# Token sums of a seven-product block FFN, formed before or after the transpose

## The chip, the cores and the metric

The kernel is one program on one core of a Trainium2 chip. The metric is the device time of one execution in microseconds (us). Engines are named as in the profile: PE (TensorE matmul) and PEld (its weight loads), DVE (VectorE), ACT (ScalarE), POOL (GpSimd), SP (SyncE, which issues most DMAs here).

## The reference, cut to what matters

One decoder layer for 1040 prompt rows (16 learned rows and 1024 tokens) and 64 sample rows, 1024 wide. It begins and ends with a SwiGLU half-step:

```python
def swiglu(x, w_gate, w_up, w_down):
    return (jax.nn.silu(x @ w_gate) * (x @ w_up)) @ w_down

def half_ffn(h, g_pre, g_post, w_gate, w_up, w_down):
    return h + 0.5 * rms_norm(swiglu(rms_norm(h, g_pre), w_gate, w_up, w_down), g_post)

h = half_ffn(h, ffn1...)                  # first half-step
...                                       # the token mixer: DeltaNet and attention
h = h + rms_norm(y @ w_out, g_mix_post)   # end of the mixer
h = half_ffn(h, ffn2...)                  # second half-step
```

Inner width is 2816. All is float32.

## The kernel before

**Seven products in place of eight.** Class `Ffn` does the products `x @ w_gate` and `x @ w_up` by a 2x2 block scheme. Tokens are cut into a left and a right half, the 1024 features into two halves of 512. Tile t = 0 to 3 (128 tokens each) is left and is paired with right tile t + 4; tile 8 is shorter, and its first half (40 tokens in the first half-step, 32 in the second) is left, its second half right. With x1, x2 the feature halves of a left tile and y1, y2 those of its right partner, the seven token operands are: 1 = x1, 2 = x2, 4 = y2, 5 = y1 + y2, 7 = x1 - y1, 6 = y1 + y2 - x1, 3 = x2 - 6. Each is kept feature-major (128 features x 4 x tokens) as a pair of fp32r tiles, high part and rest; a name such as `x60l` is operand 6, token part 0, the low tile. A product is three matmuls: high by high, rest by high, high by rest.

**A place.** `place` (L203 to L211) makes one operand of one tile: four PE transposes of 128 x 128 into a PSUM tile `tr` (L208; pool of four), an ACT copy that makes the high part (L210) and a DVE subtract that makes the rest (L211). `left` (L217) does two places for a left tile. `right` (L224) first forms the sums token-major (128 tokens x 512), two on DVE and two on POOL (L230), in place in the two token tiles and a tile `sum`, and then does five places. That is 2 x 5 + 5 x 5 = 35 places in each half-step.

**First half-step.** `tiles_in` (L1902) loads the token tiles, normalizes them (ACT square L81, POOL L82 and L83, DVE L90) and runs `left` and `right`. Left tiles have buffers of their own; right tiles 4, 5, 6, 7, 8 share two buffers, so tile 6 goes into that of tile 4. The PE work is `first`, the first products with operands 1 and 2, in two token parts, and then `start(1)`; `weave` puts the steps of `tiles_in` between its matmuls at given shares of the way (L1947 to L1951).

**End of the mixer and second half-step.** Class `Merge` walks the tiles in the order 0, 4, 1, 5, 2, 8, 6, 3, 7. For each it does the output projection (`tile_`, two PSUM tiles `dn` of 512 columns, 24 matmuls each, copied out by ACT at L1830 or L1827), adds the residual and normalizes (`finish`), and weaves into the projection of tile i the places of tile i - 2 (`feed`, L1781). The output tile is one of three:

```python
o = c.t(*((self.first, [P, H, P], F32R, "yh") if i % 3 == 0 else (self.pool, [P, H, P], F32R, "o")))
```

`self.first` has one buffer of that name and `o` two, so tile 5's output goes into the buffer of tile 0, and tile 8's into that of tile 1: the left partners of tiles 4 and 5, whose places were woven in just before. `h_d` in the profile is the store of a tile ahead of its last normalization, which is done in place. Tiles 2 and 8 are stored to DRAM (`kept`) and loaded again by `rest` (L1787), which does the places of 6, 3, 8 and 7 between the first matmuls of the second half-step (L2030 to L2034).

**Order.** PE follows the order in which the code emits, weaves included. The other engines' instructions are put in order by a scheduler; each engine then runs its own queue strictly in order. A token tile's buffer is free for its next user when the last reader or writer of the old one is done.

Of the kernel before, what the change touches and what calls it, by code (L numbers as in the profile page):

```python
# [18 lines left out]
P = 128  # L19
D = 1024  # L20
# [150 lines left out]
class Ffn:  # L171
# [31 lines left out]
    def place(self, psum, p, i, o, src, n):  # L203

        c, nc = self.c, self.nc
        ps = c.t(psum, [P, 4, P], tag="tr")
        for k in range(4):
            nc.tensor.transpose(ps[:, k, :n], src[:n, k * P:(k + 1) * P], c.ident[:n, :n])  # L208
        hi, lo = (x[:, :, o:o + n] for x in self.X[p][i])
        nc.scalar.copy(hi, ps[:, :, :n])  # L210
        nc.vector.tensor_tensor(out=lo, in0=ps[:, :, :n], in1=f32(hi), op=ALU.subtract)  # L211
# [4 lines left out]

    def left(self, psum, x, t):  # L217

        i, o, n = self.where(t)
        for p, h in ((1, 0), (2, 512)):  # L220
            self.place(psum, p, i, o, x[:, h:h + 512], n)
            yield

    def right(self, pool, psum, x, y, t):  # L224

        nc = self.nc
        i, o, n = self.where(t)
        x1, x2, y1, y2 = x[:n, 0:512], x[:n, 512:], y[:n, 0:512], y[:n, 512:]
        s = self.c.t(pool, [P, 512], tag="sum", bufs=2)[:n]
        op = lambda e, out, a, b, o: e.tensor_tensor(out=out, in0=a, in1=b, op=o)  # L230
        op(nc.vector, s, y1, y2, ALU.add)
        op(nc.vector, y1, x1, y1, ALU.subtract)
        op(nc.gpsimd, x1, s, x1, ALU.subtract)
        op(nc.gpsimd, x2, x2, x1, ALU.subtract)
        for p, src in ((4, y2), (5, s), (7, y1), (6, x1), (3, x2)):
            self.place(psum, p, i, o, src, n)
            yield
# [1453 lines left out]
class Merge:  # L1691
# [76 lines left out]
    def finish(self, t, n, o, dump):  # L1768
# [8 lines left out]
        if t in (2, 8):  # L1777
            self.kept[t] = c.t(self.f2_d, [P, D], tag="kept", bufs=2)
            nc.sync.dma_start(self.kept[t][:n], o[:n])

    def feed(self, t):  # L1781

        if t in (4, 5):
            return self.f2.right(self.pool, self.f2.ptr, self.o[t - 4], self.o[t], t), 5
        return self.f2.left(self.f2.ptr, self.o[t], t), 2

    def rest(self):  # L1787
# [5 lines left out]
        for x, src in ((x2, self.kept[2]), (x8[:n], self.kept[8][:n]), (y8[:n], self.kept[8][n:2 * n])):  # L1793
            self.nc.sync.dma_start(x, src)
        yield from right(pool, self.f2.ptr, x2, self.o[6], 6)
        yield from self.feed(3)[0]
# [371 lines left out]
```

## Time and profile before

| | us |
|---|---|
| median of 3 runs | 2686.57 (2686.21 to 2691.09) |
| profiled execution | 2687.11 |
| its span | 2685.2 |
| mean granted TensorE clock | 0.991 |
| PE busy in the span | 2604.9 (97%) |
| DVE, ACT, POOL busy | 1556.6 (58%), 1127.4 (42%), 1290.1 (48%) |

The span is the time from the first to the last instruction that the profiler sees; the 1.9 us between it and the execution's time lie outside. Rows of the timeline give the start, the duration, the engine, the line of the code, output<-inputs and the size; in brackets stands how long the engine was idle before and what released it.

### The profile page before, as it was taken

The numbers are of one execution on the slowest core, as the hardware profiler recorded it, in microseconds if no ns is written. First come the engines' busy times: TensorE is split into PE (matmuls) and PEld (weight loads), VectorE is DVE, ScalarE is ACT, GpSimd is POOL, SyncE is SP. The second block draws the span as 40 slices with busy tenths as digits, with TensorE's granted clock in tenths as the row PEclk, the third lists the DMA queues.
The fourth block names the chain that finished last, engine by engine and source line by source line (L and its number), as shares of the span: only waits on it lengthen the run. The fifth ranks groups of instructions, "written<-read, shape, count | busy, mean of one in ns | idle before, by whom it ended". The sixth has DMA issues, their size and how long they took to land. (4 is left out here: it accounts for less than half of the span.)

```text
span 2685.2 us, 49482 instructions
## 1 busy us (share of the span) xinstructions
PE 2604.9 (97%) x19053; PEld 2483.4 (92%) x19053; DVE 1556.6 (58%) x2295; ACT 1127.4 (42%) x2720; POOL 1290.1 (48%) x1223
## 2 busy tenths in 40 slices
PE   7999999999989998999999999998999999999998
PEld 7999999999988997888889999997789999999998
DVE  7656565545676669945454444443556656554566
ACT  6333343422145633566444444454443334334221
POOL 6656555445535733433343333344556555554471
PEclk9999999999999999999999999999999999999999
DMA  4343343667544753454333333334433434338764
GB/s 162 115 156 144 133 166 116 242 227 253 189 141 140 221 164 111 124 176 118 98 100 90 91 97 95 99 107 142 141 125 138 154 128 160 123 137 318 242 224 143
DMA packets 229568, 406.46 MB, mean 151 GB/s; under 512 B 59750, under 2 KB 121350, under 8 KB 229046
## 3 DMA queue, kind: packets, MB, share of 16 engines
q1 hardware_dynamic: 209030, 324.75, 37.2%
q10 hardware_dynamic: 20304, 78.56, 7.4%
q8 instruction: 150, 2.46, 0.4%
q14 instruction: 84, 0.69, 0.1%
HBM read 264.36 MB, written 140.53 MB: 151 GB/s over the span
## 5 line engine op out<-in xcount | busy, mean ns | idle before, releaser
L132 PE MATMUL gu<-xh,wl 128*128 128x512 f32 (+3 forms) x1456 | 495.4, 340 | 0.0
L128 PE MATMUL gu<-xh,wh 128*128 128x512 f32 (+3 forms) x1456 | 492.9, 339 | 0.0
L130 PE MATMUL gu<-xl,wh 128*128 128x512 f32 (+3 forms) x1456 | 492.2, 338 | 0.0
L282 POOL TENSOR_TENSOR wl<-T,wh 128x512 fp32r<-128x512 f32 x246 | 330.5, 1349 | 321.6 <-ACT wh L281 247.5
L492 PE MATMUL y<-hb,wh 128*128 128x256 f32 (+2 forms) x2528 | 430.5, 290 | 2.9 <-DVE acc L503 1.3
L282 POOL TENSOR_TENSOR wl<-raw,wh 128x512 fp32r<-128x512 f32 x200 | 282.8, 1422 | 254.3 <-ACT wh L281 193.3
L492 PEld LDWEIGHTS y<-hb,wh 128*128 128x128 f32 x2528 | 365.8, 188 | 4.3 <-DVE acc L503 1.8
L281 ACT CAST wh<-T 128x512 fp32r<-128x512 f32 x246 | 152.5, 620 | 368.7 <-PE B L316 115.5
L128 PEld LDWEIGHTS gu<-xh,wh 128*128 128x128 f32 x1456 | 278.0, 191 | 16.6 <-issue 0.9
L130 PEld LDWEIGHTS gu<-xl,wh 128*128 128x128 f32 x1456 | 278.0, 191 | 16.5 <-issue 0.4
L132 PEld LDWEIGHTS gu<-xh,wl 128*128 128x128 f32 x1456 | 278.0, 191 | 16.4 <-issue 0.4
L492 PE MATMUL y<-hb,wl 128*128 128x256 f32 (+2 forms) x1264 | 271.7, 288 | 0.2 <-POOL wl L282 0.2
L281 ACT CAST wh<-raw 128x512 fp32r<-128x512 f32 x200 | 122.3, 620 | 280.7 <-PE C L316 84.0
L503 DVE TENSOR_TENSOR acc<-acc,y 128x552 f32<-128x552 f32 (+4 forms) x216 | 144.9, 679 | 138.8 <-PE y L492 138.3
L765 POOL TENSOR_TENSOR wl<-raw,wh 128x1024 fp32r<-128x1024 f32 x60 | 145.5, 2425 | 159.9 <-ACT wh L764 130.4
L492 PEld LDWEIGHTS y<-hb,wl 128*128 128x128 f32 x1264 | 207.0, 188 | 0.5 <-POOL wl L282 0.5
L256 DVE TENSOR_TENSOR T<-raw,raw 128x512 f32<-128x512 f32 x124 | 119.9, 972 | 113.3 <-POOL wl L282 113.3
L1548 POOL TENSOR_TENSOR f<-f,mhalf 128x1 f32<-128x1 f32 (+1 forms) x72 | 54.5, 757 | 128.0 <-DVE f L1546 126.5
L267 DVE TENSOR_TENSOR T<-raw,T 128x512 f32<-128x512 f32 x62 | 64.5, 1042 | 65.1 <-POOL wl L282 64.7
L923 DVE SCALAR_TENSOR_TENSOR cv<-pc,cw,cv 128x1131 f32<-128x1131 f32 x48 | 66.8, 1393 | 31.0 <-POOL cv L920 30.7
L256 DVE TENSOR_TENSOR T<-raw,T 128x512 f32<-128x512 f32 x62 | 63.2, 1028 | 33.2 <-POOL wl L282 33.1
L1064 DVE TENSOR_TENSOR la<-la,ltmp 72x14 f32<-72x14 f32 (+37 forms) x76 | 75.3, 991 | 1.4
(592 smaller groups left out, 7304.8 us busy)
## 6 DMA issues: line engine op xcount, KB each, us to landing
hb<-hid SPq DMA_DIRECT2D x71, 552.0 KB
hb<-hid SPq DMA_DIRECT2D x71, 544.0 KB
hid<-hs ACTq DMA_DIRECT2D x69, 552.0 KB
hid<-hs ACTq DMA_DIRECT2D x69, 544.0 KB
raw<-in_w_in_dram SPq DMA_DIRECT2D x58, 512.0 KB
raw<-in_ffn_w_gate_dram SPq DMA_DIRECT2D x100, 256.0 KB
raw<-in_ffn_w_up_dram SPq DMA_DIRECT2D x94, 256.0 KB
raw<-in_ffn_w_down_dram SPq DMA_DIRECT2D x88, 256.0 KB
```

Source lines behind the costliest of these rows:

```text
L128: nc.tensor.matmul(ps, wh, xh, start=first and i == 0, stop=False)
L130: nc.tensor.matmul(ps, wh, xl, start=False, stop=False)
L132: nc.tensor.matmul(ps, wl, xh, start=False, stop=last and i == n - 1)
L256: pin(self.nc.vector.tensor_tensor(out=b[name], in0=b[x], in1=b[y], op=ALU.subtract))
L267: nc.vector.tensor_tensor(out=s, in0=b["21"], in1=s, op=ALU.subtract)
L281: self.nc.scalar.copy(hi, s)
L282: self.nc.gpsimd.tensor_tensor(out=lo, in0=s, in1=f32(hi), op=ALU.subtract)
L492: self.nc.tensor.matmul(self.view(ps[d], (i,)), w[x][:, d * P:(d + 1) * P], hb[:, y, lo:hi], start=j + x + y == 0, stop=j == len(items) - ...
L503: dve = lambda out, x, y: nc.vector.tensor_tensor(out=out, in0=x, in1=y, op=ALU.add)
L765: nc.gpsimd.tensor_tensor(out=lo, in0=raw, in1=f32(hi), op=ALU.subtract)
L923: nc.vector.scalar_tensor_tensor(out=cv, in0=pc[:, w:w + PADW], scalar=self.cw[:, j, w:w + 1], in1=cv, op0=ALU.mult, op1=ALU.add)
L1064: nc.vector.tensor_tensor(out=a[:n, 0:j, j + 1:size], in0=a[:n, 0:j, j + 1:size], in1=t, op=ALU.add)
```

## The change

Both half-steps get it at once. `left` copies each transposed half back on chip with one more ACT copy (L230 of the changed kernel), over the half of the token tile that it came from, so that the buffer of a left tile then holds it feature-major. `right` transposes y2 and y1 alone. It forms 7 = x1 - y1 and 6 = y2 - 7 on DVE, over the buffer of the right tile, and 5 = x1 + 6 and 3 = x2 - 6 on POOL, over the buffer of the left tile (all L239), all feature-major; their high and low parts are made from these SBUF tiles by the same ACT copy (L213) and DVE subtract (L214) as before. A right tile has 2 places with transposes in place of 5, and 2 steps to be woven in. The weaves are spread anew, and `kept` holds tiles 2 and 8 feature-major, stored from `left` and not from `finish`; the right half of tile 8 is stored by itself (`kept_y`).

```diff
     def left(self, psum, x, t):
         i, o, n = self.where(t)
-        for p, h in ((1, 0), (2, 512)):
-            self.place(psum, p, i, o, x[:, h:h + 512], n)
+        for p, h, own in zip((1, 2), (0, 512), self.halves(x, n)):
+            ps = self.turned(psum, x[:, h:h + 512], n)
+            self.place(p, i, o, ps)
+            self.nc.scalar.copy(own, ps)
             yield
...
-        s = self.c.t(pool, [P, 512], tag="sum", bufs=2)[:n]
...
-        op(nc.vector, s, y1, y2, ALU.add)
-        op(nc.vector, y1, x1, y1, ALU.subtract)
-        op(nc.gpsimd, x1, s, x1, ALU.subtract)
-        op(nc.gpsimd, x2, x2, x1, ALU.subtract)
-        for p, src in ((4, y2), (5, s), (7, y1), (6, x1), (3, x2)):
-            self.place(psum, p, i, o, src, n)
-            yield
+        y2 = self.turned(psum, y[:, 512:], n)
+        self.place(4, i, o, y2)
+        yield
+        y1 = self.turned(psum, y[:, 0:512], n)
+        op(nc.vector, s3, x1, y1, ALU.subtract)
+        op(nc.vector, s2, y2, s3, ALU.subtract)
+        op(nc.gpsimd, x1, x1, s2, ALU.add)
+        op(nc.gpsimd, x2, x2, s2, ALU.subtract)
+        self.place(7, i, o, s3)
+        self.place(6, i, o, s2)
+        self.place(5, i, o, x1)
+        self.place(3, i, o, x2)
+        yield
...
-        weave((first, 0, 1, 49), (steps_of(tr, 10), 0.1, 0.9, 10))
-        weave((f1.start(1, False), 0, 1, 49), (steps_of(tr, 10), 0.1, 0.9, 10))
+        weave((first, 0, 1, 49), (steps_of(tr, 4), 0.1, 0.9, 4))
+        weave((f1.start(1, False), 0, 1, 49), (steps_of(tr, 4), 0.05, 0.85, 4))
...
-        weave((steps_of(first, 48), 0, 1, 48), (steps_of(rest, 7), 0.25, 0.95, 7))
-        weave((first, 0, 1, 49), (steps_of(rest, 5), 0.1, 0.8, 5))
-        weave((f2.start(1, False), 0, 1, 49), (steps_of(rest, 5), 0.1, 0.8, 5))
+        weave((steps_of(first, 48), 0, 1, 48), (steps_of(rest, 4), 0.25, 0.9, 4))
+        weave((first, 0, 1, 49), (steps_of(rest, 2), 0.2, 0.7, 2))
+        weave((f2.start(1, False), 0, 1, 49), (steps_of(rest, 2), 0.1, 0.6, 2))
```

**First place: the loads of tiles 6, 7 and 8 in the first half-step.** SP's queue before, from the last early weight tile on; the brackets name whom a load waits for. `x_416`, `x_515` and `x_614` are tiles 6, 7 and 8.

```order
L249 DMA raw_492<-in_ffn_w_up_dram 128x512 [waits DMAHW7_49,Pool_49]
L249 DMA raw_494<-in_ffn_w_up_dram 128x512 [waits DMAHW0_49,Pool_49]
L1911 DMA x_416<-in_x_prompt_dram 128x1024 [waits DMAHW1_49,DVE_49,PE_49]
L1911 DMA x_515<-in_x_prompt_dram 128x1024 [waits DMAHW2_49,DVE_49,PE_49]
L1915 DMA x_614<-in_x_sample_dram 24x1024 [waits DMAHW3_49,DVE_49,PE_49]
L1916 DMA x_614<-in_meta_tokens_dram 16x1024 [waits DMAHW4_49]
```

The same rows of the changed kernel (tiles 6, 7 and 8 are `x_413`, `x_493` and `x_578`):

```order
L264 DMA raw_470<-in_ffn_w_up_dram 128x512 [waits DMAHW7_49,Pool_49]
L264 DMA raw_472<-in_ffn_w_up_dram 128x512 [waits DMAHW0_49,Pool_49]
L1933 DMA x_413<-in_x_prompt_dram 128x1024 [waits DVE_49,DMAHW1_49,PE_49,Pool_49]
L1933 DMA x_493<-in_x_prompt_dram 128x1024 [waits DVE_49,DMAHW2_49,PE_49,Pool_49]
L1937 DMA x_578<-in_x_sample_dram 24x1024 [waits DVE_49,DMAHW3_49,PE_49,Pool_49]
L1938 DMA x_578<-in_meta_tokens_dram 16x1024 [waits DMAHW4_49]
```

Each load now waits for POOL too: the buffer of tile 4 is read by POOL's sums, where before PE's transposes and a DVE sum were its last readers. POOL's queue at this place before, where `x_36` and `x_37` are tiles 0 and 1, `x_159` is tile 4 and `x_161` tile 5:

```order
L230 TENSOR_TENSOR x_36_139<-sum_355,x_36_139 128x512
L230 TENSOR_TENSOR x_36_139<-x_36_139 128x512
L230 TENSOR_TENSOR x_37_141<-sum_424,x_37_141 128x512
L282 TENSOR_TENSOR wl_555<-raw_492,wh_554 128x512
L230 TENSOR_TENSOR x_37_141<-x_37_141 128x512
L282 TENSOR_TENSOR wl_607<-raw_490,wh_606 128x512
```

And in the changed kernel:

```order
L297 TENSOR_TENSOR wl_521<-raw_470,wh_520 128x512
L297 TENSOR_TENSOR wl_569<-raw_468,wh_568 128x512
L239 TENSOR_TENSOR x_36_139<-x_36_139,x_159 128x512 x2
L297 TENSOR_TENSOR wl_615<-raw_472,wh_614 128x512
L239 TENSOR_TENSOR x_37_141<-x_37_141,x_161 128x512 x2
```

The sums of tile 4 (x2: two in a row) moved behind two weight splits `wl` (of the third and second weight tile) that stood behind both of them before, and they now read what PE has transposed and DVE has subtracted.

**Second place: the end of tile 4's places in Merge.** ACT's queue before. `o_21931` is tile 1's output, `yh_22017` tile 5's, in the buffer that was tile 0's; `tr` are the transposed halves.

```order
L210 CAST x40h_21779<-tr_22057 128x4x128
L210 CAST x50h_21794<-tr_22068 128x4x128
L81 ACTIVATE res_21998,rn_22007<-o_21931 128x1024
L210 CAST x70h_21804<-tr_22078 128x4x128
L210 CAST x60h_21789<-tr_22088 128x4x128
L1830 COPY yh_22017<-dn_22018 128x512
L210 CAST x30h_21774<-tr_22099 128x4x128
L1830 COPY yh_22017<-dn_22044 128x512
```

ACT's queue in the changed kernel, where `yh_21687` is tile 0's buffer, `o_21789` tile 4's, `yh_21949` tile 5's output in the buffer of `yh_21687`:

```order
L213 CAST x40h_21709<-tr_21987 128x4x128
L213 CAST x70h_21734<-o_21789 128x4x128
L213 CAST x60h_21719<-o_21789 128x4x128
L213 CAST x50h_21724<-yh_21687 128x4x128
L213 CAST x30h_21704<-yh_21687 128x4x128
L1853 COPY yh_21949<-dn_21950 128x512
L1853 COPY yh_21949<-dn_21976 128x512
```

The first copy of tile 5's output out of `dn` stood ahead of the copy for operand 3; it now stands behind it, and takes the buffer from which operands 5 and 3 are made. DVE's queue at the same place before:

```order
L619 SCALAR_TENSOR_TENSOR o_21931<-o_21931,rp_22000,g_mix_norm_post_21838 128x1024
L211 TENSOR_TENSOR x40l_21780<-tr_22057,x40h_21779 128x4x128
L211 TENSOR_TENSOR x50l_21795<-tr_22068,x50h_21794 128x4x128
L211 TENSOR_TENSOR x70l_21805<-tr_22078,x70h_21804 128x4x128
L90 SCALAR_TENSOR_TENSOR o_21931<-o_21931,rn_22007,g_ffn_norm_pre_21847 128x1024
L211 TENSOR_TENSOR x60l_21790<-tr_22088,x60h_21789 128x4x128
L211 TENSOR_TENSOR x30l_21775<-tr_22099,x30h_21774 128x4x128
```

And in the changed kernel:

```order
L214 TENSOR_TENSOR x40l_21710<-tr_21987,x40h_21709 128x4x128
L90 SCALAR_TENSOR_TENSOR o_21861<-o_21861,rn_21939,g_ffn_norm_pre_21777 128x1024
L239 TENSOR_TENSOR o_21789<-yh_21687,tr_22002 128x512
L239 TENSOR_TENSOR o_21789<-tr_21987,o_21789 128x512
L214 TENSOR_TENSOR x70l_21735<-o_21789,x70h_21734 128x4x128
L214 TENSOR_TENSOR x60l_21720<-o_21789,x60h_21719 128x4x128
L214 TENSOR_TENSOR x50l_21725<-yh_21687,x50h_21724 128x4x128
L214 TENSOR_TENSOR x30l_21705<-yh_21687,x30h_21704 128x4x128
```

The two sums (L239) stand behind the normalization L90 of tile 1 (`o_21861`), which waits for that tile's store, and ahead of all that is made from them. Before, tile 4's sums were ahead of all its places. PE meets the copy at its tile 2 (`dn_22046`), six matmuls behind the transposes of y1 (`tr_22002`):

```order
L132 MATMUL dn_21976<-xh_3933_21415,yl_21856 128x512
L207 MATMUL tr_22002<-ident_62,o_21789 128x128 x4
L128 MATMUL dn_21976<-xh_3981_21582,yh_21857 128x512
L130 MATMUL dn_21976<-xl_3982_21583,yh_21857 128x512
L132 MATMUL dn_21976<-xh_3981_21582,yl_21856 128x512
L128 MATMUL dn_21976<-xh_3981_21582,yh_21857 128x512
L130 MATMUL dn_21976<-xl_3982_21583,yh_21857 128x512
L132 MATMUL dn_21976<-xh_3981_21582,yl_21856 128x512
L128 MATMUL dn_22046<-xh_3892_21263,yh_21945 128x512
```

Before, one more place of tile 4 stood in these matmuls. The same pattern holds for tile 5's places and the output of tile 8, which goes into tile 1's buffer.

56 lines of the change are left out of this document (33 added, 23 removed).

## The prediction

> **What bounds the kernel now.** I read the page's engine rows first, then PE's waits, then the timeline at the stages in which the places lie (13 to 70 us, and 1870 to 1985 us).
>
> ```profile
> span 2685.2 us, 49482 instructions
> PE 2604.9 (97%) x19053; PEld 2483.4 (92%) x19053; DVE 1556.6 (58%) x2295; ACT 1127.4 (42%) x2720; POOL 1290.1 (48%) x1223
> PE tr L208 <- DVE x L90: 10.9, 2, 9.5
> PE tr L208 <- DVE x41l L211: 2.2, 1, 2.2
> PE tr L208 <- POOL x-8_45_157 L230: 1.8, 2, 0.9
> ```
>
> PE is the bound: it is busy for 97% of the span, and its waits on the places are few (total, count, longest): the first normalization, 2.2 us on `x41l`, 1.8 us on POOL's sums of tile 8. So what comes off PE's queue comes off the time, one for one, as long as no new wait takes its place; the other engines count only where PE waits for them.
>
> **What goes: thirty places.** Three places of each right tile, five right tiles, two half-steps. The price of one, from the timeline of tile 4 in Merge:
>
> ```profile
> 1883.64 0.40 PE L132 MATMUL dn<-xh,yl 128*128 128x512 f32 x1
> 1883.87 0.39 PE L128 MATMUL dn<-xh,yh 128*128 128x512 f32 x1
> 1884.10 0.60 PE L208 MATMUL tr<-ident,o 128*128 128x128 f32 x4
> 1884.46 0.48 PE L130 MATMUL dn<-xl,yh 128*128 128x512 f32 x1
> 1884.77 0.39 PE L132 MATMUL dn<-xh,yl 128*128 128x512 f32 x1
> ```
>
> Matmuls follow one another by 0.23 us. Four transposes hold the queue for 0.36 (1884.10 to 1884.46), and the matmul behind them takes 0.31 to the next, 0.08 more than usual: 0.44 us a place. Thirty are 13.2 us: 6.6 in the first half-step, 2.6 in Merge (tiles 4 and 5), 4.0 in the start of the second half-step. POOL's and DVE's work stays about what it was, and ACT gains 20 copies of about 0.6 (below), 12 us on an engine that is busy for 42%; I cost them at nothing, except where a chain runs through ACT.
>
> **What comes in: a longer chain behind the second transpose.** Before, the sums were made before the places, and a place was over when PE, ACT and DVE had read `tr`. Now, behind the transposes of y1, stand DVE twice, POOL twice, then ACT and DVE for operands 5 and 3; and the buffers of both token tiles are busy until that is done. The rows of the old sums (min/median/max in ns):
>
> ```profile
> L230 DVE TENSOR_TENSOR x<-x,x x4: 685/934/1668, 28.4 to 48.4; 128x512 f32<-128x512 f32 x4
> L230 POOL TENSOR_TENSOR x<-sum,x x4: 1292/1454/2278, 29.3 to 49.7; 128x512 f32<-128x512 f32 x4
> L230 POOL TENSOR_TENSOR o<-o x2: 1282/1284/1287, 1908.8 to 1971.4; 128x512 f32<-128x512 f32 x2
> ```
>
> So I take 0.68 for a DVE sum (0.60 for one right behind another), 1.25 to 1.28 for a POOL sum; the bounds above are 1.67 and 2.28, where the two engines ran beside each other. Who waits for the end of that chain? Two kinds of buffer.
>
> **Merge, tile 5's output.** It goes into tile 0's buffer, from which operands 5 and 3 of tile 4 are now made.
>
> ```profile
> 1889.12 0.60 PE L208 MATMUL tr<-ident,yh 128*128 128x128 f32 x4
> 1889.42 1.28 DVE L90 SCALAR_TENSOR_TENSOR o<-o,rn,g_ffn_norm_pre 128x1024 f32<-128x1024 f32 x1 [0.48 <-DMA h_d<-o]
> 1889.75 0.59 ACT L1830 COPY yh<-dn 128x512 f32<-128x512 f32 x1 [0.78 <-PE tr L208]
> 1890.23 0.59 ACT L210 CAST x30h<-tr 128x512 fp32r<-128x512 f32 x1
> 1890.39 0.19 PEld L128 LDWEIGHTS dn<-xh,yh 128*128 128x128 f32 x1 [0.41 <-ACT yh L1830]
> 1890.62 0.68 DVE L211 TENSOR_TENSOR x60l<-tr,x60h 128x512 fp32r<-128x512 f32 x1
> 1891.22 0.68 DVE L211 TENSOR_TENSOR x30l<-tr,x30h 128x512 fp32r<-128x512 f32 x1
> ```
>
> Now: PE's last transposes end, the copy out of `dn` follows, and PE goes on with tile 2 at 1890.39, after 0.41 us of waiting. With the change, PE has six matmuls (1.4 us) between the transposes of y1 and tile 2's first. The copy stands behind: two DVE sums (1.28), two POOL sums (2.5), `x30h` (0.59), `x30l` (0.68), the copy itself, and handovers: 6.5 us from the end of the transposes, so PE waits for at least 4.7 us with nothing else in the way. DVE has L90 of tile 1 ahead of the sums, and that waits for a store that lands at about 1889.4; it ends at 1890.7 at the earliest. From there 1.3 + 2.5 + 0.6 + 0.7 + 0.6 and handovers end at about 1896.7, where PE without the wait would be at about 1889.0 (three places earlier than now). I take 7.7 us, 0.4 of which is there already: +7.3; bounds 4.3 and 9 (slower sums).
>
> **Merge, tile 8's output.** The same with tile 1's buffer and operands 5 and 3 of tile 5.
>
> ```profile
> 1912.60 0.59 ACT L1827 COPY o<-dn 128x512 f32<-128x512 f32 x1 [0.98 <-PE tr L208]
> 1913.24 0.50 PE L128 MATMUL dn<-xh,yh 128*128 128x512 f32 x1 [0.25 <-ACT o L1827]
> ```
>
> Here four matmuls (0.9 us) stand between the transposes of y1 and tile 6's first, and no store: 5.1 by the chain, less about 0.7 of waits that go (0.25 here, 0.44 at this tile's first place): +4.4, bounds 3.5 and 7 (normalization of tile 2 stands in POOL's queue ahead of the sums).
>
> **First half-step, tile 6.** Its load goes into tile 4's buffer.
>
> ```profile
> 33.90 5.10 SPq L1911 DMA_DIRECT2D x<-in_x_prompt_dram  x2
> 37.38 1.06 ACT L81 ACTIVATE dump<-x 128x1024 bf16<-128x1024 f32 x1 [0.54 <-DMA x<-in_x_prompt_dram]
> 38.89 0.55 POOL L83 TENSOR_TENSOR rn<-rn,mhalf 128x1 f32<-128x1 f32 x1
> 39.65 1.28 DVE L90 SCALAR_TENSOR_TENSOR x<-x,rn,g_ffn_norm_pre 128x1024 f32<-128x1024 f32 x1
> 41.24 0.28 PE L316 MATMUL A<-x10h,wh 128*128 128x256 f32 x1
> 42.89 0.30 PE L316 MATMUL A<-x11h,wh 128*128 128x296 f32 x1
> 43.03 0.60 PE L208 MATMUL tr<-ident,x 128*128 128x128 f32 x4
> 59.27 0.41 PE L208 MATMUL tr<-ident,x 40*128 40x40 f32 x4 [0.33 <-DVE x L230]
> 60.53 0.44 PE L208 MATMUL tr<-ident,x-8_45_157 40*128 40x40 f32 x4 [0.86 <-POOL x-8_45_157 L230]
> 61.88 0.44 PE L208 MATMUL tr<-ident,x-8_45_157 40*128 40x40 f32 x4 [0.90 <-POOL x-8_45_157 L230]
> ```
>
> Now the load is issued at 33.90, lands after 3.5, and square, POOL and L90 end at 40.9, 2 us before PE wants the tile. With the change the load waits for POOL's second sum: y1 of tile 4 transposed, 1.3 + 2.5 + 3.5 (load) + 1.2 (square) + 0.8 (POOL) + 1.3 (L90) and handovers are 11 us. PE has only 39 matmuls and two places from there to tile 6's transposes. At 0.13 a matmul (41.24 to 42.89 is 13 of them) and 0.44 a place, with the hold of y1's own transposes, that is 6.3 us. The wait is 4.7 at the least and 6 as I take it, with a weight split (1.28) ahead on POOL. Tile 7 has the time; tile 8 is one load later still, and POOL's queue has tile 7's sums ahead of its normalization. Now PE waits 2.1 us in all at tile 8 (0.33, 0.86 and 0.90); I expect 2 to 4 more, less what its three places give, and take +2. The own copies of tiles 2 and 3 delay the start by about 0.4. Sum: -6.6 + 6 + 2 + 0.4 = +1.8 before the clock.
>
> **Start of the second half-step.** A gap that PE has now should go:
>
> ```profile
> 1955.18 0.68 DVE L230 TENSOR_TENSOR yh<-yl,yh 32x512 f32<-32x512 f32 x1 [3.00 <-DMA yl<-kept]
> 1957.80 1.01 PE L208 MATMUL tr<-ident,yl 128*128 128x128 f32 x4 [2.23 <-DVE x41l L211]
> 1955.00:1958.00 3.00, 0.77 (x7) 0.60 (x7) 2.82 (x4) 0.59 (x1) 2.01 (x1) 0.98 0.00 0
> 1958.00:1961.00 3.00, 3.00 (x16) 3.00 (x15) 2.13 (x4) 2.13 (x3) 2.92 (x3) 0.50 0.02 5
> ```
>
> DVE's sum of tile 8 waits for the load of `kept` at the head of its queue, and `x41l` of tile 6, and PE with it, behind that. In the changed order that sum stands behind tile 8's transposes, after all of tile 6 and 3. So about 2.4 us of gap go. The last two rows are windows (length, busy of PE, PEld, DVE, ACT and POOL, granted clock, DMA): after the gap PE is busy at a clock of 0.50 for some 3.3 us, which costs 1.65. That goes too: -4.1. New waits are possible, the store and load of tile 8 in pieces of 128 bytes among them, for which no row exists; I bound them by 0 and by today's gap (2.4) and take 1.0, the nearer row for a load that is wanted later.
>
> **The clock.** By the same two rows each new wait of over 2.4 us costs 1.65 us behind it: three such waits, +5. The Trainium skill (TensorE: Matmul & The Clock Gate, part 1 on what is actually happening) says that the clock halves after an idle window of about 3.4 us and comes back after as long a busy one. The 0.50 rows agree with the way back, but not with the way down: 2.4 us without work were enough here, so the row decides.
>
> **The sum.** First half-step +1.8 + 1.65; Merge -2.6 + 7.3 + 4.4 + 3.3; start of the second -4.0 - 4.1 + 1.0. That is +3.5 + 12.4 - 7.1 = +8.8. The profiled execution took 2687.1, which is 0.5 above the median of 2686.6; against the median this gives 2695.4, and I say 2695. Waits at their upper bounds (+1.7, +2.6, +2 at tile 8, +1.4) give about 2703; at their lower bounds (-3, -0.9, -1.3, -1) about 2689.
>
> A rule of the Trainium skill speaks against the change: SBUF — State Buffer, who interferes with whom, has DVE with two SBUF inputs and POOL lock each other out for a whole instruction. The subtracts that make operands 7, 6, 5 and 3 now read SBUF twice; before, one input was `tr`. The DVE row above (685 to 1668 for two SBUF inputs, beside POOL) bears it out; by the rule a POOL sum on each of the three chains would wait for one subtract, some 0.7 each, an estimate, and the sum would be 2 us higher. It stays within the range.
>
> **Rivals.**
> - *Only the places count.* The copies and loads turn out early enough, because something ahead of the chain (tile 1's store, the splits on POOL) is done sooner, and PE has no new wait over a microsecond. Then -13.2 - 4.1 and up to 3 of small waits: about 2672. For it: ACT and DVE are busy for half of the span at most. Against it: the three floors (4.3, 3.5, 4.7) come from durations alone, with no queue in them. It decides for faster from the point at which the three waits, clock included, come to under 8 us in sum; I expect 22.7 (7.3 + 4.4 + 6 + 5).
> - *The floors alone.* Each wait at its floor, and the clock not halved, or once: -13.2 - 4.1 + 4.3 + 3.5 + 4.7 + 3 + 1.65 = 0: about 2686, no change that can be told.
> - *The chain is worse.* POOL's sums at 2.28 and behind normalizations, tile 8's load late in both half-steps: 2704 to 2710.
>
> **How the numbers follow.** A measurement of this kernel can tell about 0.2%, 5.4 us: faster is below 2681.2, slower above 2692.0. My forecast (2689 to 2703) has a chance of 0.50, of which 0.06 lies under 2692; the floors 0.20, of which 0.03 are under 2681; only the places 0.20; the worse chain 0.10. So slower 0.54, same 0.23, faster 0.23. The range takes in about half of the case of the places alone and leaves out most of the last: 2673 to 2704; the likeliest case's own range is 2689 to 2703.
>
> **What would show it.** In the changed profile: the PE row of transposes at 160 instead of 280 instructions; a wait of PE on the copy of L1853 of 5 to 9 us at about 1889, one on L1850 of 4 to 7 some 20 us later, one on L90 of 5 to 7 at about 40 us, each with some 3 us at a clock of 0.50 behind it; no wait on `x41l`. If these waits are absent or under 2 us, the forecast is wrong by the sum of the floors, and the time is at 2672 to 2676.

## The result and the profile after

The changed kernel takes 2718.47 us (2716.25 to 2721.21, 4 runs), the kernel before 2688.66 (2686.21 to 2691.09, 4 runs) beside it: a ratio of 1.0111, with a 95% interval of 1.0094 to 1.0129. It is 30 us slower. The forecast was 2695 and slower; the direction holds, the size does not, and the time lies above the range. In all that follows, the ratios leave out one execution of 6510 us, in the experiment with everything together, which no trace here explains.

From the page of the changed kernel come the first two rows; the other four are PE's waits (line waited at, whose work is waited for, total us, times, longest).

```profile
span 2717.2 us, 49246 instructions
PE 2603.2 (96%) x18933; PEld 2481.7 (91%) x18933; DVE 1565.2 (58%) x2295; ACT 1137.0 (42%) x2740; POOL 1289.2 (47%) x1223
...
PE tr L207 <- DVE x L90: 20.4, 3, 9.7
PE dn L128 <- ACT o L1850: 8.7, 1, 8.7
PE tr L207 <- issue: 7.7, 1, 7.7
...
PE dn L128 <- ACT yh L1853: 5.8, 1, 5.8
```

PE has 120 instructions less, 19053 to 18933, as the thirty places of four transposes give. Yet its busy time is only 1.7 us shorter. Four waits are new: 7.6 of the 20.4 on L90 at tile 6 (9.7 is the first start, 3.1 is tile 2), 7.7 put down to "issue" at tile 8, and the two copies out of `dn`. The wait on `x41l` is gone.

Where the 30 us lie is read by stages, each from one instruction to the same instruction in the other kernel: the first half-step, the mixer, and Merge with the start of the second half-step. First the three windows of the kernel before, then of the changed one (window, length, busy time and count of PE, PEld, DVE, ACT and POOL, granted clock, DMA share, GB/s).

```profile
13.61:112.31 98.70, 89.27 (x676) 86.98 (x677) 74.35 (x95) 48.45 (x92) 64.45 (x54) 0.95 0.38 129
112.31:1852.65 1740.34, 1698.32 (x12192) 1602.36 (x12190) 997.40 (x1617) 772.77 (x2103) 792.42 (x816) 0.99 0.44 143
1852.65:2050.09 197.44, 191.18 (x1188) 169.41 (x1189) 111.12 (x124) 85.09 (x149) 105.81 (x92) 0.99 0.41 138
```

```profile
14.13:128.72 114.59, 90.04 (x616) 87.87 (x617) 77.49 (x95) 53.83 (x102) 63.79 (x54) 0.85 0.33 111
128.72:1873.34 1744.62, 1698.77 (x12191) 1602.32 (x12189) 995.12 (x1617) 772.39 (x2103) 794.42 (x816) 0.99 0.44 142
1873.34:2080.97 207.63, 188.37 (x1129) 166.76 (x1129) 118.46 (x124) 89.66 (x159) 103.37 (x92) 0.95 0.40 130
```

The first half-step is 15.9 us longer, the mixer 4.3, the last stage 10.2. Length less PE's busy time is PE's idle time: 9.4 before and 24.6 after in the first half-step (+15.1), 6.3 and 19.3 in the last (+13.0). PE's busy time should have fallen by 6.6 in each (15 places of 0.44); it rose by 0.8 in the first and fell by 2.8 in the last. The missing 7.4 and 3.8 are put down to the clock, 0.95 to 0.85 and 0.99 to 0.95. A second count agrees roughly: PE's work at half clock rose from 8.5 to 24.3 us in the first half-step and from 3.4 to 12.7 in the last stage, and half of the growth is 7.9 and 4.7. One trace of each kernel is compared here. In the second traces (last experiment) the three differences are 13.6, 3.5 and 6.3 us, above all because the kernel before took 3.8 us more in its last stage.

The new waits, from the timeline of the changed kernel (start, duration, engine, line, operation; in brackets the idle time before and its releaser). First, tile 6 in the first half-step.

```profile
38.64 1.30 POOL L297 TENSOR_TENSOR wl<-raw,wh 128x512 fp32r<-128x512 f32 x1 [1.40 <-ACT wh L296]
39.89 3.45 POOL L239 TENSOR_TENSOR x<-x,x 128x512 f32<-128x512 f32 x2
40.41 1.77 DVE L214 TENSOR_TENSOR x60l<-x,x60h 128x512 fp32r<-128x512 f32 x1
43.37 6.11 SPq L1933 DMA_DIRECT2D x<-in_x_prompt_dram  x2
47.34 1.05 ACT L81 ACTIVATE dump<-x 128x1024 bf16<-128x1024 f32 x1
50.13 1.27 DVE L90 SCALAR_TENSOR_TENSOR x<-x,rn,g_ffn_norm_pre 128x1024 f32<-128x1024 f32 x1
51.55 1.09 PE L207 MATMUL tr<-ident,x 128*128 128x128 f32 x4 [7.58 <-DVE x L90]
```

The load is issued when POOL's two sums end, at 43.37 (before: 33.90), and the transposes of tile 6 stand at the end of that chain. The two sums took 3.45 us, not 2.5, and a DVE subtract beside them 1.77, not 0.68. Tile 8 repeats this: its load waits for POOL's sums of tile 6, and POOL's sums of tile 7 then stand between the two halves of its normalization (L82 and L83). Another 2.0 us pass from the end of L83 (70.91) to L90, in which DVE works off other operations ahead of it. The next rows of the same timeline:

```profile
65.53 1.06 ACT L81 ACTIVATE dump<-x 40x1024 bf16<-40x1024 f32 x1 [1.64 <-DMA x<-in_meta_tokens_dram]
67.03 2.93 POOL L239 TENSOR_TENSOR x<-x,x 128x512 f32<-128x512 f32 x2
69.92 0.99 POOL L83 TENSOR_TENSOR rn<-rn,mhalf 40x1 f32<-40x1 f32 x1
72.88 1.27 DVE L90 SCALAR_TENSOR_TENSOR x<-x,rn,g_ffn_norm_pre 40x1024 f32<-40x1024 f32 x1
74.25 1.05 PE L207 MATMUL tr<-ident,x 40*128 40x40 f32 x8 [7.74 <-issue]
```

Then Merge: tile 5's output in tile 0's buffer, and tile 8's in tile 1's.

```profile
1907.49 1.28 DVE L90 SCALAR_TENSOR_TENSOR o<-o,rn,g_ffn_norm_pre 128x1024 f32<-128x1024 f32 x1
1910.25 3.30 POOL L239 TENSOR_TENSOR yh<-yh,o 128x512 f32<-128x512 f32 x2 [3.50 <-DVE o L239]
1914.23 0.69 DVE L214 TENSOR_TENSOR x30l<-yh,x30h 128x512 fp32r<-128x512 f32 x1
1915.59 0.79 PE L128 MATMUL dn<-xh,yh 128*128 128x512 f32 x1 [5.75 <-ACT yh L1853]
...
1935.92 3.26 POOL L635 TENSOR_TENSOR o<-o,res 128x1024 f32<-128x1024 f32 x1 [1.45 <-issue]
1937.14 0.60 PE L207 MATMUL tr<-ident,yh 128*128 128x128 f32 x4
1939.21 1.06 ACT L81 ACTIVATE res<-o 128x1024 f32<-128x1024 f32 x1 [2.45 <-POOL o L635]
1940.27 0.60 ACT L213 CAST x70h<-yh 128x512 fp32r<-128x512 f32 x1
1941.24 3.14 POOL L239 TENSOR_TENSOR o<-o,yh 128x512 f32<-128x512 f32 x2
1943.18 2.28 DVE L90 SCALAR_TENSOR_TENSOR o<-o,rn,g_ffn_norm_pre 128x1024 f32<-128x1024 f32 x1
1945.99 0.68 DVE L214 TENSOR_TENSOR x30l<-o,x30h 128x512 fp32r<-128x512 f32 x1
1947.34 0.80 PE L128 MATMUL dn<-xh,yh 128*128 128x512 f32 x1 [8.66 <-ACT o L1850]
```

In each, PE starts again 0.7 us after `x30l` has read the old tile for the last time (1914.92 to 1915.59, 1946.67 to 1947.34). At tile 8's output, POOL's residual sum of tile 2 (L635) and ACT's square of it (L81) stand in the queues ahead of the copies for operands 7 to 3, and DVE's normalization of tile 2 (L90, 2.28 us beside POOL's sums) stands ahead of the low halves of operands 5 and 3.

The clock behind these waits, from windows of the changed kernel (columns as above), in the order tile 6, tile 5's output, tile 8's output:

```profile
51.50:55.00 3.50, 3.45 (x16) 3.48 (x17) 0.19 (x1) 1.65 (x4) 0.75 (x2) 0.50 0.15 60
1914.00:1921.00 7.00, 5.41 (x13) 4.25 (x14) 2.67 (x4) 3.04 (x6) 1.88 (x3) 0.51 0.16 45
1938.70:1941.40 2.70, 0.00 (x0) 0.00 (x0) 0.99 (x2) 2.17 (x4) 1.35 (x4) 1.00 0.48 194
1941.40:1951.60 10.20, 4.26 (x10) 3.39 (x11) 5.96 (x6) 2.31 (x4) 2.98 (x2) 0.50 0.20 51
```

The clock goes down during the wait, 2.7 us after PE has stopped at tile 8's output, and stays at 0.50 for some 4 us of work after it. All stretches at half clock in the first traces of the two kernels last 3.41, 6.83 or 10.24 us, multiples of 3.41, apart from the one that the end of the trace cuts off. In the first half-step they come to 10.2 us before and 34.1 after, in the last stage to 3.4 and 20.5.

### The profile page after: what moved, and what is told of

The parts are those of the page before. It is cut to its first block, busy times and chain, and to the rows that moved or that the text cites. A ratio compares the mean times of both kernels' runs of the same rounds, so it can differ in the third digit from the quotient of the medians.

```text
span 2717.2 us, 49246 instructions
## 1 busy us (share of the span) xinstructions
PE 2603.2 (96%) x18933; PEld 2481.7 (91%) x18933; DVE 1565.2 (58%) x2295; ACT 1137.0 (42%) x2740; POOL 1289.2 (47%) x1223
## 5 line engine op out<-in xcount | busy, mean ns | idle before, releaser
L296 ACT CAST wh<-T 128x512 fp32r<-128x512 f32 x246 | 152.3, 620 | 368.0 <-PE B L331 112.2
L938 DVE SCALAR_TENSOR_TENSOR cv<-pc,cw,cv 128x1131 f32<-128x1131 f32 x48 | 66.8, 1394 | 34.4 <-POOL cv L935 34.1
L1077 DVE TENSOR_TENSOR ltmp<-la 72x14 f32<-72x14 f32 (+37 forms) x76 | 69.9, 919 | 13.1 <-DMA la<-b_d 11.5
```

Source lines behind the costliest of these rows:

```text
L296: self.nc.scalar.copy(hi, s)
L938: nc.vector.scalar_tensor_tensor(out=cv, in0=pc[:, w:w + PADW], scalar=self.cw[:, j, w:w + 1], in1=cv, op0=ALU.mult, op1=ALU.add)
L1077: nc.vector.tensor_tensor(out=t, in0=a[:n, 0:j, j:j + 1].to_broadcast([n, j, w]), in1=a[:n, j:j + 1, j + 1:size].to_broadcast([n, j, w]), ...
```

## The experiments

The experiments ran in groups on several chips, each group with the kernel before beside it (medians of 2687.69 to 2691.92 us). A difference from the changed kernel's 2718.47 is therefore good to some 3 us; the ratio to the kernel before is the safer number.

**One half-step at a time.** The first kernel makes the new sums in the first half-step alone, the second in the second half-step alone; the other half-step has the old methods and the old weave tables.

```
-                    yield from f1.right(ptr, xs[...], xs[t], t)
+                    yield from f1.right_o(xin, ptr, xs[...], xs[t], t)     # old sums; and f1.left_o
-        weave((first, 0, 1, 49), (steps_of(tr, 4), 0.1, 0.9, 4))
+        weave((first, 0, 1, 49), (steps_of(tr, 10), 0.1, 0.9, 10))
```

(That is the core of the second kernel's edit, against the changed kernel. The first is the kernel before, given the new methods and weave tables in the first half-step alone.)

> The new token sums in the first half-step alone; Merge and the second half-step as before. Theory (two buffers for the right token tiles make tile 6's and tile 8's loads wait for the new chain; the matmuls behind each wait run at half clock): the first half-step ends some 16 us late, and the kernel takes 16 to 20 us more than before. Rival (the loss lies in Merge, whose waits are as long, and the first half-step's lateness is taken up again later in the mixer): under 6 us more than before.

> The new token sums in Merge and the second half-step alone; the first half-step as before. Theory (two output tiles wait for the buffers of tiles 0 and 1): waits of PE of about 5.8 and 8.7 us at the same two copies, with about 17 us more at half clock, less the places saved: 9 to 13 us more than before. Rival (the two half-steps' waits are linked, one shifting the other): the sum of this and the run with the first half-step alone misses the 30 us of the full change by more than 5 us.

Measured: 2714.29 with the first half-step alone, ratio 1.0091 (1.0075 to 1.0108); 2699.28 with the second alone, 1.0039 (1.0024 to 1.0053). So 26.6 and 11.6 us against 2687.69 on that chip: both halves of the change cost time, the first more (26.6 where 16 to 20 were expected, 11.6 where 9 to 13 were). The waits stay with their half: 8.0 at tile 8 and none at the copies in the one, 8.8 and 5.7 at the copies and none at tile 6 in the other. The sum of the two, 38, is 8 more than the whole, so the second expectation's rival (the halves are linked, by more than 5 us) is met in the number. In the first kernel's trace 7 us stand in its last stage, whose code was the old one: 204.7 us there against 197.4, with 2.6 us of waiting for `x11h` instead of 1.0 and 13.7 us at half clock instead of 3.4. The kernel before does much the same in its second trace (201.2 us, 2.6 and 10.2), so this need not be a link between the halves. That trace is of the fastest of the four runs (2709.65); the rest of the 8 is not explained.

**Another buffer for the token tiles.** The loads of tiles 6 to 8 get buffers of their own; nothing else is changed.

```
-    tag=f"x{t}" if t in order[:5] else "x", bufs=1 if t in order[:5] else 2)
+    tag=f"x{t}" if t in order[:5] else "x", bufs=1 if t in order[:5] else 4)
```

> The changed kernel with four buffers in place of two for the right token tiles of the first half-step, so that the loads of tiles 6 and 7 wait for nothing and that of tile 8 for tile 4 alone. Theory (buffers): the waits of 7.6 and 7.7 us at tiles 6 and 8 go, and with them most of the 34 us at half clock there; the kernel gains 15 to 22 us on the changed one (2697 to 2703). Rival (the engines' queues: the sums, high and low parts are late in any case, and the normalizations of tiles 6 and 7, now early, stand ahead of the left tiles' work): PE waits as long in other places, and the gain is under 7 us.

Measured: 2706.35, ratio 1.0066 (1.0051 to 1.0081), 12 us less than the changed kernel, where 15 to 22 were expected. The first half-step falls from 114.6 to 104.3 us. Tile 6's wait is gone, and tile 8 is loaded in time; a new wait takes the place of the other, in PE's waits of this kernel:

```profile
PE B L331 <- DVE x L239: 7.0, 1, 7.0
```

Tile 8 is transposed at 56.16 now, but DVE reaches its first sum only at 63.46: seven sums and subtracts of tiles 6 and 7 and one product of the gate stand ahead of it in DVE's queue. So the buffer was the cause of the two waits for loads, and what stands behind the buffer is DVE's queue.

**Another buffer for the outputs of Merge.** Tiles 5 and 8 no longer go into the buffers of tiles 0 and 1.

```
-  o = c.t(*((self.first, [P, H, P], F32R, "yh") if i % 3 == 0 else (self.pool, [P, H, P], F32R, "o")))
+  o = c.t(*((self.first, [P, H, P], F32R, "yh") if order[i] == 8 else (self.pool, [P, H, P], F32R, "o", 3)))
```

> The changed kernel with one more output buffer in Merge: tile 5's output no longer goes into tile 0's buffer nor tile 8's into tile 1's; the order of PE is unchanged. Theory (buffers): the waits of 5.8 and 8.7 us go, with 13 us of half clock and more (6.5 us); the gain on the changed kernel is 17 to 23 us. Rival (the chain of sums is what is slow, and the next user of its results, the next tile's places or the products with operands 5 and 3, waits instead): gain under 8 us.

Measured: 2699.88, ratio 1.0037 (1.0024 to 1.0051), 18.6 us less than the changed kernel. Its last stage, in a window:

```profile
1876.51:2065.68 189.17, 182.00 (x1128) 161.73 (x1127) 116.26 (x124) 88.37 (x159) 106.57 (x92) 1.00 0.43 141
```

Without the two waits the stage takes 189.2 us: 18.5 less than in the changed kernel, and 8.3 less than in the one before. The clock is full throughout. So the whole loss of this stage is the two reused buffers, with the clock they bring down; the removed places and the closed gap are worth nearly what they should be.

**The clock by itself.** Matmuls that nobody reads fill the two places where PE waits longest in Merge: 20 into a spare bank ahead of tile 2, 30 ahead of tile 6. The waits on the copies themselves are left as they are.

```
+    fill = {2: 20, 6: 30}.get(order[i], 0)
+    if fill:
+        spare = c.t(f2.ptr, [P, 4, P], tag="tr").rearrange("p k t -> p (k t)")
+        for _ in range(fill):
+            c.nc.tensor.matmul(spare, self.w[2][0][:, :P], self.w[2][1][:, :512], start=True, stop=True)
```

> The changed kernel with matmuls into a spare bank ahead of Merge's tile 2 (20 of them, 4.7 us) and tile 6 (30, 7 us), where PE waits for the two copies; their results are not used. They add 11.7 us of PE work inside waits of 5.8 and 8.7 us. Theory (half of the loss in Merge is the clock, which is halved after each wait): the waits shrink to about 1 and 2 us, Merge and the start of the second half-step run at half clock for under 7 us instead of 20.5, and the kernel takes 5 to 9 us less than the changed one. Rival (the waits alone cost the time, the half clock is hidden in them): the same time within 2 us.

Measured: 2707.73, ratio 1.0063 (1.0046 to 1.008), 10.7 us less than the changed kernel (5 to 9 were expected), though PE was given 11.7 us of work more.

```profile
13.25:125.77 112.52, 88.10 (x616) 85.72 (x617) 77.75 (x95) 53.73 (x102) 63.99 (x54) 0.88 0.35 115
1870.94:2072.44 201.50, 195.21 (x1179) 172.75 (x1177) 118.89 (x124) 89.62 (x159) 103.64 (x92) 0.99 0.41 132
```

The last stage is 6.1 us shorter than the changed kernel's, at a clock of 0.99 instead of 0.95; its time at half clock falls from 20.5 us to 3.4. But not all of the 6.1 is the clock. With the unused matmuls in the program, the scheduler also put the other queues in another order at tile 8's output: POOL's sums stand ahead of the normalization of tile 2, two of ACT's copies ahead of its square, and DVE's L90 behind the low half of operand 3. The transposes of y1, DVE's L90 and the restart of PE in this kernel:

```profile
1932.07 0.60 PE L207 MATMUL tr<-ident,yh 128*128 128x128 f32 x4
1939.86 1.27 DVE L90 SCALAR_TENSOR_TENSOR o<-o,rn,g_ffn_norm_pre 128x1024 f32<-128x1024 f32 x1
1940.61 0.50 PE L128 MATMUL dn<-xh,yh 128*128 128x512 f32 x1 [0.18 <-ACT o L1850]
```

From the transposes to the restart pass 8.54 us, in the changed kernel 10.20 (1937.14 to 1947.34). These 1.7 us are the order of the queues. The other 4.4 fit the clock: PE's work at half clock in this stage falls from 12.7 to 3.4 us, and half of that is 4.7. Of the rest between the two traces 2.1 us stand in the first half-step and 2.4 behind this stage, where both kernels have the same code; the second trace of the changed kernel is 1.2 us shorter in the first half-step and 0.8 behind this stage without any edit, so part of that is scatter.

**The sums 5 and 3 on DVE.** POOL is taken out of the chain.

```
-        op(nc.gpsimd, x1, x1, s2, ALU.add)
-        op(nc.gpsimd, x2, x2, s2, ALU.subtract)
+        op(nc.vector, x1, x1, s2, ALU.add)
+        op(nc.vector, x2, x2, s2, ALU.subtract)
```

> The changed kernel with the sums for operands 5 and 3 on DVE in place of POOL. Theory (POOL's two sums take 3.4 us because DVE's subtracts, which read SBUF twice, run beside them, and those take 1.7 in place of 0.7): the chain is some 2 us shorter behind each pair, the four large waits lose 1.5 to 3 us each, and the kernel gains 7 to 13 us on the changed one. Rival (DVE's queue is what the chain waits in, and two more sums lengthen it): within 3 us of the changed one.

Measured: 2707.68 (2702.08 to 2713.48), ratio 1.0065 (1.004 to 1.0089), 10.8 us less than the changed kernel, inside the 7 to 13 that were expected. From the timeline of this kernel, at the places of tiles 4 and 5:

```profile
39.77 0.68 DVE L214 TENSOR_TENSOR x60l<-x,x60h 128x512 fp32r<-128x512 f32 x1
39.90 1.70 POOL L297 TENSOR_TENSOR wl<-raw,wh 128x512 fp32r<-128x512 f32 x1 [1.80 <-DVE x70l L214]
44.35 1.28 DVE L239 TENSOR_TENSOR x<-x,x 128x512 f32<-128x512 f32 x2
```

The same subtract that took 1.77 us beside POOL's sums takes 0.68 here, and two sums take 1.28 (tile 5) or 2.12 (tile 4, beside a weight split on POOL) instead of 3.45. The first half-step is 7.7 us shorter. Tile 6's wait falls from 7.6 to 5.8 and tile 8's from 7.7 to 2.8, but 2.7 us of a new wait on DVE's sums follow it. Of Merge's two waits the first falls from 5.8 to 4.6; the second stays at 8.7, where the residual sum and the square of tile 2 still stand ahead of the sums. By the Trainium skill (SBUF — State Buffer, who interferes with whom) a DVE instruction with two SBUF inputs contends with a POOL instruction that reads SBUF, and the port pair that they share is an exclusive lock. The rows agree with it: the subtract took 1.77 us when POOL's sums had begun 0.52 us before it, and 0.68 here, where POOL's split begins 0.13 us after it and takes 1.70 instead of the 1.30 of the split in the trace of the changed kernel (38.64).

**The own copies later.** The copies of tiles 0 and 1 that stay on chip go behind the squares of tiles 2 and 3 in ACT's queue.

```
-            self.nc.scalar.copy(own, ps)
+            if late is None:
+                self.nc.scalar.copy(own, ps)
+            else:
+                late.append((own, ps))
```

(The rest of the edit makes the copies in `late` behind `norm(3)`.)

> The changed kernel with the four own copies of tiles 0 and 1 behind the squares of tiles 2 and 3 on ACT. Theory (these copies delay tile 2's normalization, and the first products of the second token part come 4.6 us later for it): that part starts 2 to 4 us earlier, and the kernel gains as much. Rival (the delay is made up by the places saved and by the wait for tile 6, which starts with tile 6's load in any case): gain under 1.5 us.

Measured: 2715.72, ratio 1.0094 (1.0079 to 1.0109), 2.8 us less than the changed kernel. Counted from the first product, the first train of the second token part comes 1.5 us later than in the kernel before, where the changed kernel is 4.1 later (4.6 on the clock, as its start is 0.5 later). From there the 2.6 us are lost again: the first half-step takes 113.2 us, against 114.6 and 113.4 in the two traces of the changed kernel. So ACT's copies do delay that train, by far more than the 0.4 that was taken, and they are not what the end hangs on. The number lies in the theory's 2 to 4, but the traces bear out the rival.

**The second half-step alone, with the output buffer.**

> The new token sums in Merge and the second half-step alone, with the extra output buffer: tiles 5 and 8 no longer wait for tiles 0 and 1. Theory (without its buffer waits the change gives back the 15 places and the gap at the second half-step's start): 6 to 12 us faster than before, 2676 to 2682. Rival (the 12 us by which this half-step was slower come from the chain and not from the buffers): within 4 us of before or slower.

Measured: 2680.0 (2679.58 to 2683.88) against 2690.62, ratio 0.9964 (0.9951 to 0.9977): faster than both kernels. It is the second experiment with the edit of the fourth.

```profile
1856.37:2048.12 191.75, 184.74 (x1128) 164.50 (x1127) 119.87 (x124) 88.38 (x159) 105.50 (x92) 0.98 0.43 141
```

The last stage takes 191.8 us, against 197.4 and 201.2 in the two traces of the kernel before. The change's own gain is there once a buffer is found for the outputs.

**Everything together.** Both buffers, the sums on DVE, the late copies, and the right tiles' places earlier in the last table of the first half-step (0.03 to 0.75 of the stage, in six steps).

> The change in both half-steps with all that helped: four buffers for the right token tiles, the extra output buffer in Merge, the sums for operands 5 and 3 on DVE, the own copies of tiles 0 and 1 late, and all six places of tiles 6, 7 and 8 woven into the first 75% of the last matmuls of the first half-step (so that tile 8's chain has cover). Theory (the loss is buffers, the chain's length and the cover behind it, and no price of the change itself): the first half-step ends 2 to 6 us earlier than before, the second 8 to 10 earlier; 2674 to 2682. Rival (DVE, which has 25 more operations in a row in the first half-step, becomes what PE waits for at the end of it): the first half-step ends 3 us or more later than before, and the kernel is no faster than with the second half-step alone (2680).

Measured: 2691.15 against 2691.92, ratio 0.9993 (0.9983 to 1.0003): no change that can be told, where 2674 to 2682 was expected. In the first half-step the kernel is 8.8 us ahead of the one before at the first product with operand 6, and then loses it. Its wait there and two windows around it:

```profile
PE B L334 <- ACT x61h L213: 3.9, 1, 3.9
...
54.00:58.00 4.00, 0.31 (x1) 0.31 (x2) 4.00 (x8) 0.94 (x2) 0.06 (x1) 0.78 0.66 226
58.00:62.00 4.00, 1.84 (x7) 1.51 (x7) 4.00 (x11) 2.34 (x5) 0.00 (x0) 0.50 0.00 0
```

DVE is busy for all of these 8 us and PE for 2.2. The sums of three tiles now stand together at the end, on the engine that also makes every low half. So in the first half-step there is no gain to be had by these edits: it takes 101.0 us against 98.7. The last stage gains nothing either: it takes 196.6 us, where the output buffer with the sums on POOL gave 189.2 and 191.8.

**The best of them with the sums on DVE.**

> The change in Merge and the second half-step alone, with the extra output buffer and the sums for operands 5 and 3 on DVE. Theory (a shorter chain matters only where PE waits for its end, and with the extra buffer only the last places before the products with operands 5 and 3 do): 0 to 3 us less than with the sums on POOL (2677 to 2680), 8 to 12 less than before. Rival (DVE's queue grows): 2 us more or worse.

Measured: 2686.35 (2680.53 to 2689.79) against 2691.92, ratio 0.9977 (0.9967 to 0.9987). The gain on the kernel before is 5.6 us, where 8 to 12 were expected. The interval overlaps with that of 2680.0 (0.9964), so it can't be told whether DVE instead of POOL costs anything there; it brings nothing where no buffer waits for the chain. In the traces its last stage is the longer one, 194.3 us against 191.8.

**Both kernels once more**, for a second trace of each, with no edit.

> The kernel before, unchanged, for a second profile of it. The mixer between the half-steps, where no variant changes an instruction, took 0.2 to 8 us longer in the variants' profiles than in the first profile of before. Theory (the mixer's time scatters with the windows of the clock): this profile's mixer differs from the first one's by 1 us or more and lies in the variants' range. Rival (something in the changed kernels slows the mixer): it agrees with the first one within 0.5 us.

> The changed kernel once more, unaltered, for a second trace of it. The stage tables put 4.3 us of the 31 us of the first pair of traces in the mixer, where the change touches no instruction. If that is scatter from one execution to the next, the mixer's length from the last of the first half-step to the first of Merge differs from 1744.6 by 2 us or more and the half-clock time there from 30.7 by a window or more; if it belongs to the program, both come out as before, within 1 us. The three waits (7.6 at tile 6, 5.8 and 8.7 at the copies out of dn) belong to the program by every theory and should come back within 0.5 us each; the half-clock windows behind them may differ by one window of 3.4 us. Time 2713 to 2722.

Measured, in single runs: the kernel before 2691.16, the changed one 2715.45 (with the kernel before at 2696.87 beside it, 18.6 less). Counted from the same instructions, the mixer of the kernel before differs between its traces by about 0.2 us. That of the changed kernel is 3.8 us longer than the mixer before, where the first trace had 4.3, with 30.7 us at half clock in both. So the mixer's loss is not scatter from one execution to the next, as far as two traces of each can tell: it goes with the program. What does vary in the kernel before is the start of its second half-step: its last stage took 197.4 us in the first trace and 3.8 more in the second, with 10.2 us at half clock instead of 3.4. The waits of the changed kernel came back: 7.58 us at tile 6, 7.9 at tile 8, 5.8 and 8.7 at the copies.

## Why the prediction was right in direction and wrong in size

*What goes.* Thirty places at 0.44 us: right, as far as can be told. PE's 120 instructions are gone. The price was not measured by itself; with the output buffer, PE's busy time in the last stage falls from 191.2 to 182.0 us, 1.7 of which is the half clock that goes, and 7.5 for 15 places are 0.50 each. Where no new wait comes in (the output buffer) the last stage gains 8.3 us; the prediction's terms for it (places, gap and new small waits, -2.6 - 4.0 - 4.1 + 1.0) come to -9.7.

*The gap at the second start.* Right: the wait on `x41l` is gone, and between `dn` of tile 3 and the middle of that start the changed kernel gains 8.3 us (forecast 7.1). Another 3.8 us are lost just behind it, at the products with operands 5 and 3; the prediction's 1.0 for new waits was too small.

*The mechanism.* Right: the buffer of a left tile is read by a longer chain, and what is loaded or copied into it waits. Giving those buffers a second place takes the waits away, worth 12 and 18.6 us.

*The sizes.* The prediction's sum and the measurement, in the same parts (us; measured from the stage windows of the first pair of traces, with the places put in at the predicted -6.6 for each half-step):

| term | predicted | measured |
|---|---|---|
| first half-step, waits | +8.4 | +15.1 |
| first half-step, clock | +1.65 | +7.4 |
| Merge and second start, waits | +10.3 | +13.0 |
| Merge and second start, clock | +1.65 | +3.8 |
| mixer | 0 | +4.3 |
| places | -13.2 | -13.2 |
| sum | +8.8 | +30.4 |

Five steps failed, in order of size.

The first is the price of the first half-step's waits, 6.7 us too low. The 15.1 are 7.6 at tile 6, 7.7 less the old 2.1 at tile 8, and some 1.7 more at tile 2. Tile 6 was near (6 taken). Tile 8 was not (+2 taken): its load waits for tile 6's sums, and POOL's sums of tile 7 (2.93 us) go ahead of the end of its normalization. The prediction named that queue and did not price it. Tile 2 waits since own copies on ACT stand ahead of its square. Own copies were put at 0.4 (those of tiles 2 and 3 alone); the second train comes 4.1 us later, of which the experiment that moved four of them gave 2.6 back.

The second is the clock in the first half-step, 5.8 too low. One half-clock stretch of 3.3 us was taken for each new wait, worth 1.65. The long waits at tiles 6 and 8 brought three such stretches in a row each (10.24 us): PE's work at half clock rose from 8.5 to 24.3 us in the first half-step. The gap that the price came from was 2.4 us long and had one stretch behind it. The trace before also holds two stretches in a row, 6.83 us from 25.96 on, around waits of no more than 1.4 us each; that was a sign that one stretch per wait was no safe price.

The third, the mixer, was not in the sum at all, since no instruction of it is changed. From POOL's timeline, the same sum in the kernel before, in the changed kernel and in its second trace:

```profile
865.92 2.41 POOL L951 TENSOR_TENSOR dt<-dt,cst 128x1024 f32<-128x1024 f32 x1
...
883.57 3.61 POOL L966 TENSOR_TENSOR dt<-dt,cst 128x1024 f32<-128x1024 f32 x1
...
882.03 3.15 POOL L966 TENSOR_TENSOR dt<-dt,cst 128x1024 f32<-128x1024 f32 x1
```

Over this sum, between 857 and 874 us of the kernel before, the changed kernel falls back by 2.5 us in its first trace and 2.8 in its second, and the second trace of the kernel before does not. The cause is open. A later start alone does not explain it: the kernel with the new sums in the first half-step alone enters the mixer nearly as late as the changed one (at 128.0 us, against 128.7) and loses 0.6 there, and the one with the new sums in the second half-step and the output buffer enters it as early as the kernel before (at 112.2, against 112.3) and loses 3.9, further on. Nor does the order of the queues: DVE, ACT and POOL take the mixer's instructions in the same order in these four kernels. All other variants lose 1.6 to 8.3 us.

The fourth is Merge, with errors of both signs. At tile 5's output 7.7 was taken and 5.75 measured: L90 of tile 1 did not wait for its store (it runs at 1907.49, ahead of the sums), and POOL's 3.30 for two sums instead of 2.5 ate part of that. At tile 8's output 5.1 was taken and 8.66 measured: the normalization of tile 2, which was kept for the upper bound of 7, holds ACT's copies and DVE's last subtracts as well as POOL's sums. The fifth is the clock there, two and three stretches behind those waits instead of one each, less the one that went.

*The lock between DVE and POOL.* It was given 2 us beside the sum. POOL's pair of sums took 2.93 to 3.48 in these chains instead of 2.5, and the experiment without POOL was 10.8 us faster, clock and queue included. The row that the prediction showed for the old sums on POOL had a median of 1.45 us for one beside its best of 1.29 and its worst of 2.28; two at the median, 2.9, would have been a better guide than two at the best, because in the new order subtracts of operands 7 and 6 run beside POOL's sums.

*The rivals.* "Only the places count" is refuted by the four waits; with the output buffer it holds for Merge. "The floors alone" is refuted as well. "The chain is worse", which had 0.10 and 2704 to 2710, is what happened, by its own mechanism (slower sums, a normalization ahead of them, tile 8 late) and with the clock on top. The waits at tile 6 and at the two copies out of `dn` were taken near the middle of their bounds, as if they were independent. Tile 6's went to its upper end (7.6), that at tile 8's output past it (8.7 against 7), and that at tile 5's output (5.75) stayed below the 7.7 taken.

## What to carry to other kernels

When a change makes a tile's buffer be read by a longer chain, list who gets that buffer next (a load, a copy out of PSUM) and follow the chain to its last reader with the engines running side by side, not with each instruction's best time. One more output buffer here was worth 18.6 us, more than the 13.2 estimated for all the transposes that the change removed. And price a wait of TensorE with the clock that goes down during it: here 4 to 5 us of the work behind each of Merge's two waits ran at half speed.

## What the runs showed of the hardware

Half clock came in stretches of 3.41, 6.83 or 10.24 us, and at tile 8's output it began after 2.7 us without work. Filling two waits with 11.7 us of unused matmuls made their stage 6.1 us shorter, some 4.4 of it by the clock. A subtract of 128x512 on DVE took 0.68 us when POOL did not hold it up and 1.75 to 1.77 beside POOL's sums, and two of these sums took 2.93 to 3.48 us instead of 2.5.
